# A mixer in four PSUM banks, a LayerNorm in two steps, and a build whose TensorE work is spread

## The chip, the core and the metric

The kernel runs on one core of one Trainium2 chip. It is one program for all engines: PE (TensorE) multiplies matrices, DVE (VectorE), ACT (ScalarE) and POOL (GpSimd) work on vectors, SP issues most of the transfers. The metric is the device time of one execution in microseconds (us). A profiled execution is a run of its own, and its trace gives for each instruction the start, the length, and what ended the idle time ahead of it.

## What is computed

The reference is one decoder layer on 512 prompt tokens and 32 sample tokens (8 sequences of 4), with 1,024 features, in f32. Cut to what matters:

```python
proj = x @ w_in + b_in                          # q, k, v, g, ca, cg: 512 columns each
o, r_new = retention(rope(q), rope(k), v, r0)   # 4 heads of 128, chunks of 128 tokens
ret_out = silu(g) * head_norm(o)
conv_out, buf_new = conformer_conv(ca, cg, ...) # GLU, causal convolution of width 31, LayerNorm, swish
mix = concat(ret_out, conv_out) @ w_out
x = layer_norm(ALPHA * x + mix, ln1_g, ln1_b)

q = x @ w_query                                 # 8 heads, two halves of 128 each
s1, s2 = q1 @ sub_keys_1, q2 @ sub_keys_2       # 128 keys each
v1, i1 = top_k(s1, 16);  v2, i2 = top_k(s2, 16)
sv, ci = top_k(v1[:, None] + v2[None], 16)      # 16 of 256 pairs
idx = e1 * 128 + e2;  gate = softmax(sv)        # 16 of 16,384 experts per head
act = gelu(peer_u[idx] . x)
ffn = sum(gate * act * peer_v[idx])
y = layer_norm(ALPHA * x + ffn, ln2_g, ln2_b)
```

Each token uses 8 × 16 = 128 experts. An expert has a row of `peer_u` and one of `peer_v`, 4 KB each.

## The kernel before, in words

**Two ways through the experts.** For the first two blocks of 128 prompt tokens (called `x1_0` and "b") and for the samples ("s", 32 tokens, four experts of each at once, so 32 slots instead of 128) the experts are gathered. `gather` (its generator issues one slot per step) has POOL issue an indirect DMA of 128 rows of 8 KB (L579, 1 MB), DVE takes the dot product with the token (L582), ACT the Gelu and the scale by the gate (L590, L591), and DVE adds the scaled v row to an accumulator (L596). The other 256 prompt tokens (`ND`) go through all 16,384 experts densely: for each of 128 first keys `e`, `scores_of(e)` multiplies the block `ut[e]` of 128 experts with `x1T` on PE (L801, eight f32 matmuls, two records each in the trace), ACT takes the Gelu into a tile of weights `GW`, and `v_stage(e)` multiplies the weights with the v rows into the four accumulators `pB` in PSUM (L939). The weights are zero but for the chosen experts: `build` makes, for groups of 8 tokens, one-hot matrices from the top-k's results (ACT's `off` and `A`, L879 and L881; DVE's `M` and `B`, L883 and L887), multiplies them on PE (L892, 24 bf16 matmuls for a group), and DVE multiplies the result into the weights (L916) or copies it there for keys whose scores come later (L918).

The 128 first keys are in four groups: Gb (32 keys), Gc (20), Ga (44) and Gd (32). The scores of Ga and Gb are computed ahead of the build, one key after the other, each with a PSUM tile `sp` and a Gelu of its own (L847, L852); those of Gc during the first build by `s_stage`; those of Gd during the tail.

**The stages in time.** Up to about 386 us: input projections, convolution and retention, with the first 128 tokens taken right through to their top-k, so that their gather (`gather0`) runs from then on beside everything else. 386 to 454: the mixer. Blocks of w_out are loaded as `wo`; `mix_a` multiplies (L478; `residual`, L465, adds ALPHA times x), for the 32 samples and for three blocks of 128 tokens; `mix_b` normalizes (`layer_norm`, L444 to L458: statistics on DVE, the inverse root on POOL, a scalar for the shift on DVE at L454, ACT's Identity at L456, then DVE's product with g and sum with b) and has PE transpose the result (L489) into `x1T`. PSUM is in two pools, `ps` of five banks and `ps0` of three, used alternately. Then `caches` writes the convolution's caches out (two transposes, L429 and L437, and ten stores), and 470 to 785 is the retrieval: `w_query` in four units of two heads (`project`, L198), their key scores (L524), and `retrieve` on DVE (MAX8 and its companions, L506 to L510), first for the dense tokens, then for "b" and "s". The Ga and Gb scores fill PE meanwhile, up to 857. The first slots of the "s" gather run from 786; `FREE` = 12 of them may run ahead of the `fence`, the last DVE instruction of `first_keys`. 858 to 985: `first_keys`, the first build, with one `s_stage` every 12 tokens. 985 to the end, the tail: `phases` (v rows, Gd's scores and `last_keys`, the second build) and `fetched` (the remaining slots of "s" and 128 of "b") step by step beside each other, then the last LayerNorms and stores.

**What sets the order.** The program is written against tiles; a scheduler that simulates the engines sets each engine's order, which is then fixed: every engine runs its instructions in that order and each waits for its semaphores. Pools with `bufs=` n make the n+1st tile wait for the last user of the first. `behind(a, b)` keeps an instruction after another in that order without a wait of its own. `hold(k, ins)` says that the dots of `gather0` from slot k on come after `ins`; the mixer has such holds at slots 52, 56, 60, 64 and 68.

The layer's `layer_norm` before, with the instructions that the change is about:

```python
rsqrt(rs[:n, 0:1], mv[:n, 1:2])
V.scalar_tensor_tensor(rs[:n, 1:2], mv[:n, 0:1], -1.0, rs[:n, 0:1], op0=OP.mult, op1=OP.mult)
for q, c in enumerate(halves if src else [slice(0, D)]):
    S.activation(t[:n, c], src[q][:n] if src else t[:n, c], AF.Identity, bias=rs[:n, 1:2], scale=rs[:n, 0:1])
    V.tensor_mul(t[:n, c], t[:n, c], g[:n, c])
    steps["ln"] = V.tensor_add(t[:n, c], t[:n, c], b[:n, c])
```

## Time and profile before

| | |
|---|---|
| median of 3 runs | 1592.72 us (1591.25, 1592.72, 1597.43) |
| profiled execution | 1598.13 us, span 1595.8 us |
| granted TensorE clock, mean | 0.968 |
| PE, DVE, ACT, POOL busy | 94%, 77%, 38%, 23% |
| moved by DMA | 503.75 MB, mean 316 GB/s |

A row of the timeline gives start, length, engine, line, operation, output and inputs, how many such instructions stand in a row, and in brackets the idle time ahead of it with what ended it. A row of a stretch gives its length, the busy time of each engine with the number of instructions, the granted TensorE clock, the share of time that the 16 DMA engines were busy, and GB/s. The tail's records of PE overlap slightly at their ends, so a sum of single lengths is larger than the time they take.

### The profile page before, as it was taken

What the parts mean: (1) busy time and instruction counts of PE and PEld (TensorE: products, weight loads), DVE (VectorE), ACT (ScalarE), POOL (GpSimd) and SP (SyncE); (2) the same over time, 40 slices, a digit from 0 to 9 for tenths busy, and PEclk for the clock granted to TensorE, in tenths of its full rate; (3) what the DMA queues carried; (4) which work ended last, traced back from release to release, by engine and by line L of the source; (5) the groups of instructions that cost most, each with busy time, mean ns of one, the idle gap of its engine ahead of it and who ended that gap; (6) DMA issues with size and microseconds to landing.
All of it is one profiled execution on the core that took longest, in us unless ns stands there. A gap on an engine that the chain in (4) does not pass through costs nothing.

```text
span 1595.8 us, 20861 instructions
## 1 busy us (share of the span) xinstructions
PE 1499.0 (94%) x7046; PEld 1015.8 (64%) x7046; DVE 1225.1 (77%) x3158; ACT 602.9 (38%) x1686; POOL 365.0 (23%) x335
## 2 busy tenths in 40 slices
PE   7899999997969999999899997999999999999995
PEld 6788657565856668788788885444566656543332
DVE  4939998878866999999863789656877777766666
ACT  2234353145222333333533798413994111111111
POOL 2001324333331221222120001222224222222221
PEclk9899989998989999999999997999999999999998
DMA  9458787995698779999796322998999999999995
GB/s 362 176 189 346 250 301 238 353 332 208 231 377 344 274 266 342 342 344 344 268 362 238 107 93 87 393 391 328 394 359 390 424 424 423 424 424 424 423 424 209
DMA packets 99543, 503.75 MB, mean 316 GB/s; under 512 B 10183, under 2 KB 21191, under 8 KB 56549
## 3 DMA queue, kind: packets, MB, share of 16 engines
q0 software_dynamic: 42240, 305.12, 49.1%
q1 hardware_dynamic: 50749, 189.96, 31.5%
q10 hardware_dynamic: 6448, 7.36, 1.5%
q8 instruction: 55, 0.90, 0.2%
q14 instruction: 51, 0.42, 0.1%
HBM read 497.03 MB, written 5.80 MB: 315 GB/s over the span
## 4 chain that ended last, share of the span: by engine, by line
DMA 29%; PE 28%; DVE 24%; issue 9%; ACT 7%; POOL 3%; SPq 0%; DVEq 0%; POOLq 0%; ACTq 0%
DMA g<-in_uv_dram,Ib 18%; PE sp L801 9%; DMA g<-in_uv_dram,I 7%; DVE acc L596 6%; PE pB L939 5%; PE mm L198 4%; DVE g L582 4%; ACT off L879 3%; POOL g L579 2%; PE mm L478 2%; PE mm L263 2%; DMA g<-in_w_in_dram 2%; PE mm L892 2%; ACT A L881 1%; PE mm L309 1%
## 5 line engine op out<-in xcount | busy, mean ns | idle before, releaser
L801 PE MATMUL sp<-x1T,uv 128*128 128x256 f32 x2048 | 465.0, 384 | 14.2 <-ACT Ga L847 7.1
L596 DVE SCALAR_TENSOR_TENSOR acc<-g,wgt,acc 128x1024 f32<-128x1024 f32 x285 | 364.8, 1280 | 116.6 <-ACT wgt L591 113.8
L801 PEld LDWEIGHTS sp<-x1T,uv 128*128 128x128 f32 x2048 | 385.9, 192 | 87.4 <-issue 14.9
L590 ACT ACTIVATE act<-act 128x1 f32<-128x1 f32 x288 | 57.7, 200 | 574.5 <-DVE g L582 567.9
L579 POOL DMA_INDIRECT g<-in_uv_dram,I x128 | 164.9, 1288 | 468.0 <-DVE acc L596 236.0
L582 DVE SCALAR_TENSOR_TENSOR g<-g,x1g 128x1024 f32<-128x1024 f32 x160 | 195.3, 1223 | 97.1 <-DMA g<-in_uv_dram,Ib 64.3
L579 POOL DMA_INDIRECT g<-in_uv_dram,Ib x128 | 135.9, 1062 | 498.0 <-DVE acc L596 314.8
L198 PE MATMUL mm<-x1T,w 128*128 128x384 f32 (+1 forms) x512 | 178.1, 505 | 0.0
L582 DVE SCALAR_TENSOR_TENSOR g<-g,x 128x1024 f32<-128x1024 f32 x128 | 154.9, 1215 | 26.7 <-DMA g<-in_uv_dram,I 26.5
L939 PE MATMUL pB<-uv,Ga 128*128 128x512 f32 x352 | 162.1, 603 | 0.6 <-DMA uv<-in_uv_dram 0.4
L879 ACT ACTIVATE off<-row,e1T 128x128 bf16<-128x128 bf16 x512 | 157.9, 389 | 1.0
L198 PEld LDWEIGHTS mm<-x1T,w 128*128 128x128 f32 x512 | 97.9, 193 | 72.4 <-issue 41.0
L939 PE MATMUL pB<-uv,Gd 128*128 128x512 f32 x256 | 117.2, 601 | 2.1 <-DMA uv<-in_uv_dram 1.0
L939 PE MATMUL pB<-uv,Gb 128*128 128x512 f32 x256 | 115.4, 604 | 2.0 <-DMA uv<-in_uv_dram 1.4
L939 PEld LDWEIGHTS pB<-uv,Ga 128*128 128x128 f32 x352 | 63.7, 189 | 82.9 <-issue 63.1
L939 PEld LDWEIGHTS pB<-uv,Gd 128*128 128x128 f32 x256 | 46.1, 189 | 73.3 <-issue 71.5
L892 PEld LDWEIGHTS <-A 128*128 128x128 bf16 x1536 | 64.0, 99 | 34.7 <-issue 26.0
L939 PEld LDWEIGHTS pB<-uv,Gb 128*128 128x128 f32 x256 | 47.6, 192 | 58.8 <-issue 52.6
L892 PE MATMUL mm<-B,A 128*128 128x96 bf16 (+1 forms) x1536 | 67.7, 195 | 11.2 <-DVE Gc L918 10.0
L881 ACT ACTIVATE A<-off 128x1024 bf16<-128x1024 bf16 x64 | 67.4, 1053 | 22.5 <-PE mm L892 21.7
L939 PE MATMUL pB<-uv,Gc 128*128 128x512 f32 x160 | 72.3, 599 | 0.0
L887 DVE TENSOR_TENSOR B<-M,gtT 128x768 bf16<-128x768 bf16 (+1 forms) x192 | 69.5, 415 | 3.1 <-PE mm L892 3.0
(279 smaller groups left out, 1712.4 us busy)
## 6 DMA issues: line engine op xcount, KB each, us to landing
uv<-in_ut_dram SPq DMA_DIRECT2D x128, 512.0 KB
uv<-in_uv_dram SPq DMA_DIRECT2D x128, 512.0 KB
w<-in_w_in_dram SPq DMA_DIRECT2D x18, 1024.0 KB
w<-in_w_query_dram SPq DMA_DIRECT2D x16, 1024.0 KB
w<-in_w_out_dram SPq DMA_DIRECT2D x7, 1024.0 KB
g<-in_uv_dram,I POOLq DMA_INDIRECT x128
keys<-in_state_retention_dram ACTq DMA_DIRECT2D x4, 512.0 KB
out_dram<-keys SPq DMA_DIRECT2D x4, 512.0 KB
```

What stands on the lines that cost most here:

```text
L198: T.matmul(p[:, :n], w[m // 2][:, k, (m % 2) * 128:(m % 2 + 1) * 128], xT[:, k, c0:c0 + n], start=(k == 0), stop=(k == 7))
L263: T.matmul(p[:, :L], dg[:, k % 4], u_p[:, m, p0 + k:p0 + k + L], start=(k == 0), stop=(k == CK - 1))
L579: G.indirect_dma_start(out=t, out_offset=None, in_=a["uv"], in_offset=bass.IndirectOffsetOnAxis(ap=idx[:, k:k + 1], axis=0))
L582: dot = V.scalar_tensor_tensor(t[:, :D], t[:, :D], 1.0, x1, op0=OP.mult, op1=OP.mult, accum_out=act[:, 0:1])
L590: S.activation(act[:, 1:2], act[:, 0:1], AF.Gelu)
L596: V.scalar_tensor_tensor(acc, v, wgt, acc, op0=OP.mult, op1=OP.add)
L801: T.matmul(sp, u[:, k], x1T[:, k, NG2:], start=(k == 0), stop=(k == 7))
L879: S.activation(off[:, t], row, AF.Abs, bias=e1T[:, t1 + t:t1 + t + 1])
L881: S.activation(A, off, AF.Relu, bias=1.0, scale=-1.0)
L887: V.tensor_tensor(B[:, q], M, pairs_of(gtT[:, q], t1).to_broadcast([128, TB // 2, ne, 2]), op=OP.mult)
L892: T.matmul(pt[:, t % nt], A[:, t - t1], B[:, q, (t - t1) // 2, :, t % 2], start=(q == 0), stop=(q == 2))
L939: T.matmul(pB[b][q], W[:, b * 128:(b + 1) * 128], vt[:, q * 512:(q + 1) * 512], start=False, stop=(e == NK - 1), skip_group_check=True)
```

## The change

1. **LayerNorm in two steps.** DVE computes (x − mean)·g in one instruction, straight from PSUM where the source is there, and then that times the inverse deviation plus b. L454 and ACT's Identity go. The inverse root is POOL's as before, or, with `table=True` (the "b" block's and the two dense blocks' last LayerNorms), ACT's Sqrt and DVE's reciprocal.
2. **Caches and loads.** `caches()` moves ahead of the mixer. The third block of w_out goes to the space of `u_p`, and the first unit of w_query is loaded before the mixer, partly into the space of `blk`.
3. **Mixer in four banks.** `ps` and `ps0` are closed ahead of the mixer; it has four banks (`mx`), and the other four (`pq`) hold the first query unit, computed by `first_unit` in columns 0 to 160, 160 to 288 and 288 to 416 between the mixer's pieces. `mix_b(NS, C)` now precedes `mix_a(NS + C, C, 1)`. The holds are at slots 52, 54, 56, 59 and 62.
4. **Score pairs.** For Ga and Gb one PSUM tile takes two keys' scores, and one Gelu empties it.
5. **PE's work in the first build spread.** `s_stage`'s first matmul comes behind the build's matmul of its token; a stage comes every 31/3 tokens in place of 12, and after the 20 keys of Gc come the products of four v rows with the first 128 dense tokens. Their other half follows after the fence.
6. **`FREE` from 12 to 20.** Eight more slots of "s" may run ahead of the fence.

Its core:

```diff
-        rs = gw.tile([128, 2], F32, name="lrs", bufs=3)
-        rsqrt(rs[:n, 0:1], mv[:n, 1:2])
-        V.scalar_tensor_tensor(rs[:n, 1:2], mv[:n, 0:1], -1.0, rs[:n, 0:1], op0=OP.mult, op1=OP.mult)
-        for q, c in enumerate(halves if src else [slice(0, D)]):
-            S.activation(t[:n, c], src[q][:n] if src else t[:n, c], AF.Identity, bias=rs[:n, 1:2], scale=rs[:n, 0:1])
-            V.tensor_mul(t[:n, c], t[:n, c], g[:n, c])
-            steps["ln"] = V.tensor_add(t[:n, c], t[:n, c], b[:n, c])
+        rs = gw.tile([128, 1], F32, name="lrs", bufs=3)
+        if table:
+            S.activation(rs[:n], mv[:n, 1:2], AF.Sqrt, bias=eps_c[:n])
+        else:
+            rsqrt(rs[:n], mv[:n, 1:2])
+        cs = halves if src else [slice(0, D)]
+        for q, c in enumerate(cs):
+            V.scalar_tensor_tensor(t[:n, c], src[q][:n] if src else t[:n, c], mv[:n, 0:1], g[:n, c],
+                                   op0=OP.subtract, op1=OP.mult)
+        if table:
+            V.reciprocal(rs[:n], rs[:n])
+        for c in cs:
+            steps["ln"] = V.scalar_tensor_tensor(t[:n, c], t[:n, c], rs[:n], b[:n, c], op0=OP.mult, op1=OP.add)
...
-    wo = load_w(a["w_out"], 0) + load_w(a["w_out"], 512)
+    caches()
+    spare = [u_p.rearrange("p m t -> p (m t)")[:, 0:2 * D], blk[:, 0:2 * D]]
+    spare = [t.rearrange("p (k e) -> p k e", k=8) for t in spare]
+    wo = load_w(a["w_out"], 0) + load_w(a["w_out"], 512, [spare[0], None])
...
+    wq0 = load_w(a["w_query"], 0, [None, spare[1]])
+    fps.close()
+    leftp, mxs = ExitStack(), ExitStack()
+    pq = leftp.enter_context(tc.tile_pool(name="pq", bufs=4, space=PSUM, side="right", reuse_waits="tile"))
+    mx = mxs.enter_context(tc.tile_pool(name="mx", bufs=4, space=PSUM, reuse_waits="tile"))
+    banks[:] = [mx]
+    q_first = [pq.tile([128, 512], F32, name="mm") for _ in range(4)]
+
+    def first_unit(c0, c1):
+
+        for m in range(4):
+            for k in range(8):
+                T.matmul(q_first[m][:, c0:c1], wq0[m // 2][:, k, (m % 2) * 128:(m % 2 + 1) * 128], x1T[:, k, c0:c1],
+                         start=(k == 0), stop=(k == 7), skip_group_check=True)
+
     mix_a(0, NS, None)
     mix_a(NS, C, 0)
     mix_b(0, NS)
+    hold(54, steps["ln"])
+    mix_b(NS, C)
     hold(56, steps["ln"])
     mix_a(NS + C, C, 1)
-    mix_b(NS, C)
-    hold(60, steps["ln"])
     mix_a(NS + 2 * C, C, None)
+    first_unit(0, NS + C)
     mix_b(NS + C, C)
-    hold(64, steps["ln"])
+    hold(59, steps["ln"])
+    first_unit(NS + C, NS + 2 * C)
     mix_b(NS + 2 * C, C)
-    hold(68, steps["ln"])
-    caches()
+    hold(62, steps["ln"])
+    first_unit(NS + 2 * C, n)
...
+    def scores_of(e, ne=1, after=None):
+
+        sp = pdn.tile([128, 2, ND], F32, name="sp")
+        for i in range(ne):
+            u = uvp.tile([128, D], F32, name="uv").rearrange("p (k e) -> p k e", k=8)
+            nc.sync.dma_start(u, a["ut"][e + i])
+            for k in range(8):
+                p = T.matmul(sp[:, i], u[:, k], x1T[:, k, NG2:], start=(k == 0), stop=(k == 7), skip_group_check=True)
+                if after is not None and i + k == 0:
+                    behind(p, after)
+        return sp[:, 0:ne] if ne > 1 else sp[:, 0]
...
-    for e in range(E0S[2], E0S[3]):
-        S.activation(place(e), scores_of(e), AF.Gelu)
+    for e in range(E0S[2], E0S[3], 2):
+        S.activation(place2(e), scores_of(e, 2), AF.Gelu)
...
-    for e in range(EG[0]):
-        S.activation(place(e), scores_of(e), AF.Gelu)
+    for e in range(0, EG[0], 2):
+        S.activation(place2(e), scores_of(e, 2), AF.Gelu)
...
-                if ts.stop % 12 == 0 and done < EG[1]:
-                    s_stage(E0S[1] + done, ts.stop)
+                if ts.stop != 4 * ((8 + 31 * (done + len(ahead)) // 3) // 4):
+                    continue
+                if done < EG[1]:
+                    s_stage(E0S[1] + done, ts.stop, mm)
                     done += 1
+                elif len(ahead) < UV:
+                    ahead.append(v_row(len(ahead)))
+                    behind(v_products(len(ahead) - 1, ahead[-1], 0), mm)
...
     def phases():
-        for e in range(EG[0]):
+        for e, vt in enumerate(ahead):
+            v_products(e, vt, 1)
+            yield
+        for e in range(len(ahead), EG[0]):
             v_stage(e)
             yield
```

## The prediction

> **What bounds the kernel now.** I read the busy shares first, then the busy time by stage, then within each stage the rows that end its idle time.
>
> ```profile
> span 1595.8 us, 20861 instructions
> PE 1499.0 (94%) x7046; PEld 1015.8 (64%) x7046; DVE 1225.1 (77%) x3158; ACT 602.9 (38%) x1686; POOL 365.0 (23%) x335
> ```
>
> PE's 94% is a mean; the next rows give, by stretch, busy time of PE, PE weight loads, DVE, ACT and POOL, then granted clock, DMA share and GB/s.
>
> ```profile
> 450.00:470.00 20.00, 6.95 (x38) 5.77 (x37) 12.26 (x18) 4.50 (x12) 5.89 (x6) 0.66 1.01 422
> 600.00:780.00 180.00, 175.04 (x854) 152.06 (x854) 177.18 (x691) 61.85 (x160) 39.50 (x34) 0.99 0.90 330
> 785.90:857.80 71.90, 68.92 (x331) 60.20 (x330) 35.20 (x51) 25.09 (x79) 14.51 (x13) 0.98 0.95 364
> 857.80:985.70 127.90, 116.47 (x1078) 99.92 (x1077) 101.37 (x382) 107.55 (x301) 0.00 (x0) 0.93 0.27 88
> 985.70:1587.00 601.30, 587.53 (x2288) 300.94 (x2288) 424.39 (x636) 200.74 (x633) 159.41 (x153) 0.99 0.97 391
> 1400.00:1577.00 177.00, 174.27 (x383) 68.63 (x382) 119.69 (x143) 24.14 (x97) 41.26 (x44) 1.00 0.99 412
> ```
>
> So five stages bind differently: a PE stall at 450–470; the retrieval, where PE and DVE are both 97–98% busy; the rest of the scores, on PE and DMA; the build, where PE, ACT and DVE stand at 91, 84 and 79% and POOL and the DMA engines have next to nothing; and the tail, where PE is 98% busy and DMA 97%.
>
> **Mixer and first query unit.**
>
> ```profile
> 386.43 1.06 PE L478 MATMUL mm<-w,blk 128*32 128x256 f32 x2 [5.95 <-ACT blk L300]
> 438.95 13.98 PE L478 MATMUL mm<-w,blk 128*128 128x256 f32 x64
> 466.86 1.08 PE L489 MATMUL mm<-cst,xr 128*128 128x128 f32 x4 [13.05 <-DVE xr L458]
> 479.78 12.73 PE L198 MATMUL mm<-x1T,w 128*128 128x416 f32 x36
> 129.87 3.73 PE L198 MATMUL mm<-g,w 128*128 128x128 f32 x32
> 391.52 1.51 ACT L333 ACTIVATE on<-mm,hnb,hrs 128x128 f32<-128x128 f32 x4 [1.01 <-DVE hnb L330]
> 458.32 1.23 DVE L582 SCALAR_TENSOR_TENSOR g<-g,x 128x1024 f32<-128x1024 f32 x1 [5.93 <-DMA g<-in_uv_dram,I]
> 505.93 0.93 DVE L506 MAX8 vf<-score 128x8 f32<-128x128 f32 x4 [0.90 <-ACT score L527]
> ```
>
> The mixer's matmuls run from 386.43 to 452.9, and with the transposes after them to 453.8; then PE waits 13.05 us for the last LayerNorm, of which 5.93 is DVE sitting in a gather dot whose slot had not landed. Query unit 0 ends at 492.5 and the top-k begins at 505.93. The change takes the gather out of the LayerNorms and puts three pieces of query unit 0 into those waits. It doesn't get the whole 13 us. (1) In the new order the transposes of the third retention chunk (input `on`, ready at 391.52 + 1.51 = 393.0) stand ahead of all mixer matmuls, where before the mixer filled 386.4 to 393: −7 us of the gain. (2) Four banks mean that each pair waits for the LayerNorm that reads it; one such wait, 3–4 us, stands after the second block. (3) The unit whole is 64 records in 22.5 (36 in 12.73); a piece of 128 columns is 64 in 7.5 (32 in 3.73), the one of 160 a quarter more, 9.3, so the three take 24.3. Summed from 394: two mixer blocks 30 (13.98 each and 1 to 2 of residuals), wait and transposes 4.5, two blocks 32, first piece 9.3, transposes 2, two pieces and the last transposes 16: about 488. Against 492.5 that is a gain of 4.4 (bounds −9 to +3, the whole stall less 7 against a second LayerNorm wait). The score records that PE ran between unit 0 and the first top-k are only moved, not saved: the keys' load leaves its place behind the cache outputs, so the top-k can begin near 489, 17 us early.
>
> **What DVE does with 17 us.** By the order of DVE, the new mixer holds 8 gather slots where the old held 12, and 52 to 67 rather than 52 to 77 are done when the top-k begins: 10 slots move behind it.
>
> ```profile
> L596 DVE SCALAR_TENSOR_TENSOR acc<-g,wgt,acc 128x1024 f32<-128x1024 f32 x285 | 364.8, 1280 | 116.6 <-ACT wgt L591 113.8
> L582 DVE SCALAR_TENSOR_TENSOR g<-g,x 128x1024 f32<-128x1024 f32 x128 | 154.9, 1215 | 26.7 <-DMA g<-in_uv_dram,I 26.5
> L801 PE MATMUL sp<-x1T,uv 128*128 128x256 f32 x2048 | 465.0, 384 | 14.2 <-ACT Ga L847 7.1
> 786.91 1.48 DVE L887 TENSOR_TENSOR B<-M,gtT 128x768 bf16<-128x768 bf16 x3
> ```
>
> A slot is 1.22 + 1.28 = 2.5 us of DVE: 10 are 25. With DVE full in the retrieval, its chain comes to the build's first operands (before at 786.91) not 17 earlier but 25 − 17 = 8 us later.
>
> **Score pairs.** One Gelu for two keys lets PE run a pair ahead. PE's waits from 470 to 860, by what it waited for (total, times, longest):
>
> ```profile
> PE sp L801 <- ACT Ga L847: 7.1, 5, 3.1
> PE sp L801 <- ACT Gb L852: 4.7, 2, 3.0
> 857.80 0.29 DVE L916 TENSOR_TENSOR Gb<-Gb,mm 128x128 f32<-128x128 f32 x1 [12.11 <-ACT Gb L852]
> 844.40 1.28 DVE L596 SCALAR_TENSOR_TENSOR acc<-g,wgt,acc 128x1024 f32<-128x1024 f32 x1 [0.66 <-ACT wgt L591]
> ```
>
> If all 11.8 goes, PE ends the second group near 857.8 − 4.4 − 11.8 = 841. But DVE, which had 12.11 us of room before its first multiply at 857.80, comes 8 later: its twelfth slot of the s gather ends near 845.7 + 8 = 854, and the multiply follows it. The DMA engines at 0.95 cannot pull those slots in. The build therefore starts at about 853, −5 (bounds −16, both gains whole, to +4, a slot's landing later each).
>
> **Build.**
>
> ```profile
> 861.67 4.55 PE L801 MATMUL sp<-x1T,uv 128*128 128x256 f32 x20
> 866.05 1.20 PE L892 MATMUL mm<-B,A 128*128 128x96 bf16 x24
> 867.09 4.55 PE L801 MATMUL sp<-x1T,uv 128*128 128x256 f32 x20
> 899.29 0.29 DVE L916 TENSOR_TENSOR Gb<-Gb,mm 128x128 f32<-128x128 f32 x1 [1.89 <-PE mm L892]
> 973.62 2.08 PE L892 MATMUL mm<-B,A 128*128 128x96 bf16 x24 [2.23 <-DVE Gc L918]
> 966.00:985.00 19.00, 10.57 (x142) 9.61 (x143) 18.29 (x72) 18.71 (x51) 0.00 (x0) 0.64 0.01 2
> 857.80:985.70 127.90, 7.86 (x16) 2.71 (x16) 0.93 0.27 88
> L591 ACT ACTIVATE wgt<-act,GTb 128x1 f32<-128x1 f32 x128 | 37.4, 292 | 3.5
> 985.75 8.47 PE L939 MATMUL pB<-uv,Gb 128*128 128x512 f32 x16 [0.38 <-DVE Gb L916]
> ```
>
> The first groups of 8 tokens take 5.42 us (861.67 to 867.09) with PE the bound and DVE idle 1.89 in each; at the end DVE and ACT are busy 18.3 and 18.7 of 19 us, and PE waits in each group. Spreading the key scores evens this; the ideal would be the busiest engine's sum. That was PE's 116.5 of 127.9. The change adds 8 slots, 8 × 2.5 = 20, to DVE: 101.4 + 20 = 121.4; ACT gets a Gelu and a scale for each, 8 × 2 × 0.29 = 4.7 at most, 112. Four half rows of value products (16 records, as in the row of L939 in the build, 7.86 us) change nothing: the build already held 16. So DVE becomes the longest, and its queue is in order: each dot waits for its slot, each acc for two ACT instructions behind the `off` chain (0.66 in the row of 844.40), and the multiplies behind them hold the PSUM bank from PE. I take 10% over 121.4, as 127.9 stands 10% over 116.5: 134 and a slot's landing at the front, 135, +7 (bounds −4, 124, to +15, 143). The fence then falls at 853 + 135 = 988, some 2 us after 985.7.
>
> **Tail.** 8 slots fewer of 148. At 1 MB each (128 rows of 8 KB) and the 412 GB/s of 1400–1577 they are 8 × 1.05/0.412 = 20 us of DMA. PE doesn't follow:
>
> ```profile
> 985.70:1587.00 601.30, 459.04 (x1008) 183.98 (x1008) 0.99 0.97 391
> L892 PE MATMUL mm<-B,A 128*128 128x32 bf16 x768 | 24.4, 176 | 0.3 <-ACT A L881 0.3
> 1576.43 3.60 PE L939 MATMUL pB<-uv,Gd 128*128 128x512 f32 x8
> 1577.33 1.29 DVE L603 SCALAR_TENSOR_TENSOR yt<-x1g,acc 128x512 f32<-128x512 f32 x2
> 1586.93 1.45 ACT L456 ACTIVATE g<-pB,lrs 128x512 f32<-128x512 f32 x2 [2.77 <-DVE lrs L454]
> 1589.02 1.28 DVE L458 TENSOR_TENSOR g<-g,lnb 128x512 f32<-128x512 f32 x2
> ...
> 388.27 1.28 ACT L590 ACT_TABLE_LOAD   x1
> ```
>
> The first row is L939 alone in the tail: 1,008 records, whose 459 us overlap at their ends; at 8 in 3.60 less that overlap, 0.44 each, they are 444. With 24.4 for the second build and 512 score records (32 keys) at 4.38/20 = 0.22, 113, PE needs about 582 of the 594.3 us to the last matmul at 1580.0. So at most 12.3 comes back. Part of PE's idle is the tail's first rows and the join at its end, not the DMA: −9 (bounds −12.5 to −3).
>
> **End.** From 1577.33 to 1590.3 DVE alternates the LayerNorm of the last gathered block with the two dense ones, the last store ends the span 5.5 later. With DMA 20 us lighter, the gathered block ends before PE, and each dense block sheds ACT's Identity pair (1.45): −4.5 (bounds −6 to 0, a table load being the charge against it). A Sqrt needs a table other than Gelu's; a load takes the 1.28 of the row of 388.27, and can stand in the chain once, if the statistics don't cover it.
>
> The Trainium skill ("ScalarE: Activation LUTs", What ACT_TABLE_LOAD costs) adds a drain of some 1.38 us to such a load; the row agrees on the load and shows no drain by itself; by the page the end would gain 3.1 rather than 4.5.
>
> **The sum.** −5 + 7 − 9 − 4.5 = −11.5 us against the profiled execution's own 1598.1 (span 1595.8 and 2.3 around it): 1586.6. The median shown, 1592.72, stands 5.4 below that execution, so I give 1592.7 − 11.5 = 1581.
>
> **Rivals.**
> (a) Everything carries: the top-k's early start is not eaten because DVE waits less for slots (the row of L582 shows 26.5 us of DMA waits), the pairs give 10, the build stays at 128 and the tail gives 12: −10 − 4.4 − 12 − 4 ≈ −30, 1562. For it: PE's records are a fixed sum, and its idle is what the change removes. Against it: DVE's 177.18 of 180.
> (b) The change doesn't arrive at the end: the 25 us on DVE eat front and pairs (start 857), the build takes 138 and the tail returns 8: 0 + 10 − 8 − 3 ≈ −1, 1592. For it: the DVE sum of 121.4 and a tail that is PE's.
> (c) Slower: the build becomes a chain of waits. A gather dot in DVE's queue that waits for its slot holds the multiplies, PE idles in each group, and the granted clock falls, as in 966–985 (clock 0.64, 24 records 2.08 in place of 1.20). A group with a key score then needs up to 16 × 0.22 × 2.08/1.20 = 6.1 for it and 2.1 for its own matmuls, against 3.5 and 1.2; if the 20 such groups take 5.4 and the other 12 DVE's 121.4/32 = 3.8, the build is 154, +26; with −5 − 6 − 3 that is +12, 1605. It decides from a build of 127.9 + 14 + 8 = 150 on. For it: DVE becomes the longest engine and PE idles between groups; against it: the stage's mean clock of 0.93, of which its last 19 us at 0.64 leave (0.93 × 127.9 − 0.64 × 19)/108.9 = 0.98 for the rest, where the groups hold key scores.
>
> The Trainium skill ("TensorE: Matmul & The Clock Gate", Part 1: The HAM clock gate) says that TensorE's full clock has to be held by activity and that an idle window of about 3.4 us halves it. The trace agrees in direction: 0.66 beside the 13.05 us stall, 0.64 where waits of 1 to 2 us recur, though none of those is 3.4 long. By the page's threshold alone (c) would not arise from waits that short; the rows say that it can.
>
> **How the numbers follow.** The sum above: 0.46, and its own range 1574 to 1589; (a) 0.20; (b) 0.18; (c) 0.16. A difference below 0.5%, 8 us, is what a measurement of this kernel can just tell from none: 1584.7 to 1600.7 is no change. The sum's case lies below 1584.7 in 0.39 of its 0.46, (a) wholly: faster 0.59. The other 0.07 and (b)'s 0.16 are no change, 0.23; (c) and 0.02 of (b) slower, 0.18. For eight in ten the range runs from 1560, below (a), to 1602, which leaves out most of (c).
>
> **What the profile after would show.** Right: no wait above 5 us between mixer and query unit 0, its end near 488; MAX8 of the dense top-k near 490; no waits of L801's scores on Ga and Gb; the first Gb multiply at 850–855 behind a gather dot; 32 build groups of about 4.2 us; a fence at 985–990; last matmul near 1572, and 11 us behind it. Wrong: a build over 150 or under 128; a first multiply before 846 (then DVE was not the bound) or after 860; a tail shorter than 582, which would say that its PE work was smaller than I summed.

## The result, and the profile after

The changed kernel takes 1600.12 us (median of 7 runs, 1597.67 to 1605.91) against 1592.72 for the kernel before (7 runs, 1589.28 to 1601.61): a ratio of 1.0056, 95% interval 1.003 to 1.0081. Forecast were 1581 us and a gain. The profiled execution of the changed kernel took 1605.57 us, its span is 1603.6. The lines of the changed file are shifted: L939 is now L950, L801 is L833, L892 is L926, L582 is L590, L590/L591 are L598/L599, L596 is L604, L916/L918 are L966/L968, L900 is L935 and L903 is L938.

The stretches of the changed kernel that answer to those shown of before (length; busy time of PE, PE weight loads, DVE, ACT, POOL; granted clock, DMA share, GB/s):

```profile
450.00:470.00 20.00, 20.00 (x112) 18.40 (x112) 14.71 (x22) 1.99 (x8) 3.78 (x4) 1.00 0.51 191
600.00:780.00 180.00, 173.25 (x850) 151.27 (x849) 176.66 (x661) 68.36 (x158) 43.81 (x36) 0.99 0.95 351
859.30:1000.70 141.40, 120.02 (x1077) 101.11 (x1075) 118.10 (x398) 111.38 (x316) 8.39 (x8) 0.94 0.42 145
1000.70:1590.00 589.30, 582.72 (x2279) 300.43 (x2280) 398.75 (x599) 195.74 (x617) 161.70 (x139) 1.00 0.95 385
```

The stall at 450–470 is gone. The retrieval moves more (351 GB/s, before 330) with DVE as full as before. The build is 13 us longer, and no engine fills it: PE is busy for 120 of 141 us and DVE for 118. The tail stands where it stood.

For the comparison of stages I take four marks from each trace: ACT's `on` of the third retention chunk (391.52 before, 392.05 after), DVE's first multiply of the build into Gb, the first value product released by DVE behind the build (the fence), and the end of the last matmul. They don't depend on where the front began, which differs by up to 9 us between executions.

| us | on to Gb multiply | build | fence to last matmul | behind it |
|---|---|---|---|---|
| before | 466.3 | 128.0 | 594.3 | 15.8 |
| changed | 467.2 | 141.5 | 593.4 | 9.5 |
| difference | +0.9 | +13.5 | −0.9 | −6.3 |
| predicted | −5 | +7 | −9 | −4.5 |

With the 0.5 by which `on` came later the differences add to the 7.8 between the two spans.

The ends of PE's waits in the changed kernel, from 380 to 990 (total, times, longest):

```profile
PE mm L341 <- ACT on L334: 11.3, 1, 11.3
PE mm L926 <- DVE Gc L968: 10.1, 8, 3.1
PE mm L779 <- ACT x1T L498: 4.4, 1, 4.4
PE mm L868 <- DVE e L862: 4.0, 1, 4.0
PE sp L833 <- ACT act L598: 3.9, 1, 3.9
PE mm L926 <- ACT A L915: 3.8, 2, 2.6
PE sp L833 <- ACT Ga L881: 2.7, 2, 1.8
PE mm L497 <- DVE keys L466: 2.6, 1, 2.6
...
```

PE stands 11.3 us at the head of the mixer for `on`, then 2.6 for a LayerNorm (L497), 4.4 for the copy of the transposed blocks that the second piece of query unit 0 reads (L779), 4.0 for the dense top-k's result (L868), which DVE finishes late, and 3.9 and 2.7 for a score's PSUM tile that ACT has not emptied yet. Before, the list had 13.1 us for the last LayerNorm, 11.8 for the Gelus of scores and 6.0 at the head of the mixer. The first and the last went and the second fell to 6.6, but the new waits are about as long as what was saved.

And inside the build, DVE's waits of the changed kernel from 861.9 to 1000:

```profile
DVE Gc L938 <- ACT W L935: 18.0, 7, 4.8
DVE Gb L966 <- PE mm L926: 4.7, 6, 1.5
DVE acc L604 <- ACT wgt L599: 0.6, 1, 0.6
```

The 18.0 us are new. DVE waits here for no gather slot, and only 0.6 us in a slot's chain; it waits for W, the Gelu of a key score.

### The profile page after: what moved, and what is told of

Read it like the earlier page. It is cut to its first block, busy times and chain, and to the rows that moved or that the text cites. A ratio compares the mean times of both kernels' runs of the same rounds, so it can differ in the third digit from the quotient of the medians.

```text
span 1603.6 us, 20993 instructions
## 1 busy us (share of the span) xinstructions
PE 1501.4 (94%) x7174; PEld 1030.4 (64%) x7174; DVE 1222.3 (76%) x3143; ACT 587.9 (37%) x1636; POOL 377.4 (24%) x329
## 4 chain that ended last, share of the span: by engine, by line
PE 54%; DVE 27%; DMA 10%; issue 5%; ACT 3%; POOL 2%; SPq 0%; DVEq 0%; POOLq 0%; ACTq 0%
PE pB L950 27%; PE sp L833 12%; DVE acc L604 6%; DVE g L590 5%; DMA g<-in_uv_dram,I 4%; PE mm L486 4%; PE mm L199 3%; PE mm L926 2%; PE mm L264 2%; DMA g<-in_w_in_dram 2%; POOL g L587 1%; PE mm L310 1%; DVE iu L518 1%; DVE B L921 1%; DVE score L516 1%
## 5 line engine op out<-in xcount | busy, mean ns | idle before, releaser
L833 PE MATMUL sp<-x1T,uv 128*128 128x256 f32 x2048 | 472.3, 389 | 10.2 <-ACT act L598 3.9
L833 PEld LDWEIGHTS sp<-x1T,uv 128*128 128x128 f32 x2048 | 392.2, 195 | 85.6 <-issue 25.3
L604 DVE SCALAR_TENSOR_TENSOR acc<-g,wgt,acc 128x1024 f32<-128x1024 f32 x285 | 364.2, 1278 | 108.0 <-ACT wgt L599 106.5
L598 ACT ACTIVATE act<-act 128x1 f32<-128x1 f32 x288 | 57.6, 200 | 628.6 <-DVE g L590 622.3
L587 POOL DMA_INDIRECT g<-in_uv_dram,Ib x128 | 150.6, 1177 | 439.1 <-DVE acc L604 290.2
L590 DVE SCALAR_TENSOR_TENSOR g<-g,x1g 128x1024 f32<-128x1024 f32 x160 | 195.0, 1221 | 53.9 <-DMA g<-in_uv_dram,Ib 37.8
L590 DVE SCALAR_TENSOR_TENSOR g<-g,x 128x1024 f32<-128x1024 f32 x128 | 154.5, 1212 | 26.1 <-DMA g<-in_uv_dram,I 25.4
L950 PE MATMUL pB<-uv,Ga 128*128 128x512 f32 x352 | 162.2, 604 | 0.3
L199 PE MATMUL mm<-x1T,w 128*128 128x384 f32 (+1 forms) x448 | 153.3, 498 | 0.0
L199 PEld LDWEIGHTS mm<-x1T,w 128*128 128x128 f32 x448 | 84.5, 190 | 60.7 <-issue 28.6
L950 PE MATMUL pB<-uv,Gb 128*128 128x512 f32 x256 | 116.1, 606 | 5.0 <-DMA uv<-in_uv_dram 3.0
L950 PEld LDWEIGHTS pB<-uv,Ga 128*128 128x128 f32 x352 | 63.7, 190 | 83.8 <-issue 63.0
L950 PE MATMUL pB<-uv,Gd 128*128 128x512 f32 x256 | 114.8, 599 | 0.9
L950 PEld LDWEIGHTS pB<-uv,Gd 128*128 128x128 f32 x256 | 47.0, 190 | 68.7 <-issue 50.4
L926 PEld LDWEIGHTS <-A 128*128 128x128 bf16 x1536 | 61.4, 96 | 43.9 <-issue 22.7
L950 PEld LDWEIGHTS pB<-uv,Gb 128*128 128x128 f32 x256 | 47.9, 192 | 59.7 <-issue 52.6
L926 PE MATMUL mm<-B,A 128*128 128x96 bf16 (+1 forms) x1536 | 65.3, 192 | 18.3 <-DVE Gc L968 10.1
L950 PE MATMUL pB<-uv,Gc 128*128 128x512 f32 x160 | 72.8, 601 | 0.0
```

Source lines behind the costliest of these rows:

```text
L199: T.matmul(p[:, :n], w[m // 2][:, k, (m % 2) * 128:(m % 2 + 1) * 128], xT[:, k, c0:c0 + n], start=(k == 0), stop=(k == 7))
L587: G.indirect_dma_start(out=t, out_offset=None, in_=a["uv"], in_offset=bass.IndirectOffsetOnAxis(ap=idx[:, k:k + 1], axis=0))
L590: dot = V.scalar_tensor_tensor(t[:, :D], t[:, :D], 1.0, x1, op0=OP.mult, op1=OP.mult, accum_out=act[:, 0:1])
L598: S.activation(act[:, 1:2], act[:, 0:1], AF.Gelu)
L604: V.scalar_tensor_tensor(acc, v, wgt, acc, op0=OP.mult, op1=OP.add)
L833: p = T.matmul(sp[:, i], u[:, k], x1T[:, k, NG2:], start=(k == 0), stop=(k == 7), skip_group_check=True)
```

## The experiments

Each ratio is to runs of the kernel before that were taken with the run's own (medians 1593.7 to 1595.6 us). Lengths of stages come from one profiled execution of each version.

### The build: the slots, or the places of the key scores

Twelve slots in place of 20 ahead of the fence, all else as changed:

```diff
-FREE = 20
+FREE = 12
```

> The changed kernel with 12 instead of 20 slots of the s gather allowed ahead of the fence; all else as changed. In the changed kernel the build takes 141 us from the first Gb multiply (859.3) to the fence (1000.7), before 128. Theory A (the 8 slots lengthen the build by their DVE time): the build falls to 125-129, the tail, which PE bounds, stays at 593 us from fence to last matmul, the time is 1586 to 1589, against 1600 as changed. Theory B (the key scores' new places lengthen it: DVE waits 18.0 us there for W, ACT 18.4 us for PE): the build stays at 134 or more, the time is 1594 or more.

Measured: ratio to before 1.0044 (1.0027 to 1.0061), build 136.2 us, tail 593.8, end 14.7. In these two profiles the slots cost 141.5 − 136.2 = 5.3 us of build, and without them the end behind the last matmul is 5.2 longer: their account is even. DVE's waits for W are 28.2 us here against 18.0, so the slots' 20 us of DVE partly fill time in which it waits anyway.

The old places of the key scores, 20 slots:

```diff
-                if ts.stop != 4 * ((8 + 31 * (done + len(ahead)) // 3) // 4):
-                    continue
-                if done < EG[1]:
-                    s_stage(E0S[1] + done, ts.stop, mm)
+                if ts.stop % 12 == 0 and done < EG[1]:
+                    s_stage(E0S[1] + done, ts.stop)
                     done += 1
-                elif len(ahead) < UV:
-                    ahead.append(v_row(len(ahead)))
-                    behind(v_products(len(ahead) - 1, ahead[-1], 0), mm)
```

> The changed kernel with the old first build: a key score every 12 tokens with no tie to the build's matmuls, no v products ahead; 20 slots stay. Theory A (slots): the build stays at 136 to 142 us, the time at 1597 to 1602. Theory B (places of the key scores): the build falls to 126-130 although the slots are in it, DVE's waits for W go from 18 us to under 4, the time is 1586 to 1590.

Measured: ratio 0.9972 (0.9945 to 0.9999), build 130.7 us. Both edits together:

> The changed kernel with the old first build and 12 slots: only the two-step LayerNorm, the mixer with query unit 0, and the pairs are left of the change. Both theories: the build is back at 126-129 us, the fence at 986-988, the tail 593, the end 9.5 us after it as in the changed kernel (15.8 before): 1586 to 1588, faster than before by 5. If the time is at or above that of before, the front part of the change costs more than its first Gb multiply (859.3 against 857.8) shows.

Measured: ratio 0.9967 (0.9947 to 0.9988), build 125.2, tail 592.8, end 14.7. The end was expected at 9.5; what sets it is told under "End". The places of the key scores cost 141.5 − 130.7 = 10.8 us with 20 slots and 136.2 − 125.2 = 11.0 with 12. That the two agree so closely is partly luck, since the same build differs by up to 2.7 us between profiles. The table has every profile of this record with the old or the spread places and with none or all of the eight slots inside the build (the other edits of these runs lie outside it; the runs not yet named are told below):

| build, us | none of the 8 slots | all 8 |
|---|---|---|
| old places | 127.9 (before), 125.2 (both edits), 125.9 (pairs alone) | 130.7 (old places), 129.6 (the same with moved gating) |
| spread places | 136.2 (12 slots), 137.9 (light DVE), 137.9 (96 slots of the first gather) | 141.5 (changed), 140.0 (moved gating), 140.5 (32 slots of "b") |

In the runs with a light DVE and with 96 slots of the first gather, all 20 slots were done ahead of the build. By the means the places cost 11.0 and 10.5 us, and the slots 3.8 and 3.3. Theory B holds, and slots and places add. How the places cost is seen in one stretch of the changed kernel, by engine, PE first:

```profile
931.88 0.68 PE L926 MATMUL mm<-B,A 128*128 128x96 bf16 x12 [2.61 <-ACT A L915]
932.40 5.37 PE L833 MATMUL sp<-x1T,uv 128*128 128x256 f32 x16
937.60 1.19 PE L926 MATMUL mm<-B,A 128*128 128x96 bf16 x24
```

```profile
931.83 2.44 ACT L913 ACTIVATE off<-row,e1T 128x128 bf16<-128x128 bf16 x8
937.80 0.28 ACT L935 ACTIVATE W<-sp 128x132 f32<-128x132 f32 x1 [3.53 <-PE sp L833]
938.38 1.06 ACT L915 ACTIVATE A<-off 128x1024 bf16<-128x1024 bf16 x1
```

```profile
933.16 0.18 DVE L968 COPY Gc<-mm 128x32 f32<-128x32 f32 x1
938.11 0.30 DVE L938 TENSOR_TENSOR Gc<-Gc,W 128x132 f32<-128x132 f32 x1 [4.77 <-ACT W L935]
938.99 1.48 DVE L921 TENSOR_TENSOR B<-M,gtT 128x768 bf16<-128x768 bf16 x3
```

PE begins a key score at 932.40. W stands in ACT's order and its product in DVE's right behind the group's multiplies, ahead of `A` and `B` of a later group. ACT idles 3.53 us and DVE 4.77 until PE has finished that one score. While they stand, nothing is made for a later group, and PE waits in turn for `A` or for DVE's copy out of PSUM (2.61 us here for `A`, 2.58 for the copy ahead of the score at 956.59). Behind such a wait the score itself is slower, 5.37 against 3.68 for the same 16 records. Five of the 20 key scores are, each behind a wait of PE of 1.6 to 3.1 us; together they lose 7.4. The granted clock (third number from the end) shows it, in the wait, in the score's first 3.5 us, and behind the score:

```profile
929.25:931.88 2.63, 0.02 (x2) 0.03 (x2) 2.63 (x12) 2.57 (x8) 0.00 (x0) 1.00 0.60 198
932.40:935.90 3.50, 3.50 (x13) 2.85 (x11) 0.76 (x5) 1.87 (x7) 0.00 (x0) 0.55 0.02 7
937.60:940.00 2.40, 2.40 (x32) 2.25 (x31) 1.89 (x8) 2.04 (x5) 0.00 (x0) 1.00 0.47 147
```

To see whether it is the nearness or the spreading, the spread places were kept and only the use of a score was put one stage later:

```diff
-                if ts.stop != 4 * ((8 + 31 * (done + len(ahead)) // 3) // 4):
+                if ts.stop != 4 * ((8 + 31 * (done + len(pend) + len(ahead)) // 3) // 4):
                     continue
+                if pend:
+                    s_use(*pend.pop(), ts.stop)
+                    done += 1
                 if done < EG[1]:
-                    s_stage(E0S[1] + done, ts.stop, mm)
-                    done += 1
+                    pend.append((E0S[1] + done, scores_of(E0S[1] + done, 1, mm)))
```

Here `s_use` is the rest of `s_stage`, the Gelu and the product, and `pend` holds the score that is not used yet.

> The changed kernel with the key scores of the first build where it has them (tied behind the build's matmuls, spread), but their Gelu and the product with the weights one stage, some 10 tokens, later. Theory B in its narrow form (DVE's and ACT's waits for a score that PE has only just begun are what costs): DVE's waits for W fall from 18 us to under 4 and the build from 141.5 to 129-132, ratio 0.997 to 0.999. Theory G (the cost is PE's: a score between the groups holds the next group's matmuls and the idle in between lowers its clock): the build stays at 137 or more, ratio 1.003 to 1.006.

Measured: build 130.5 us, ratio 0.9987 (0.9957 to 1.0017) against 1.0056. The stretch of the build of this run:

```profile
858.00:988.50 130.50, 113.77 (x1078) 96.10 (x1076) 117.73 (x398) 110.79 (x316) 8.95 (x8) 0.99 0.46 158
```

DVE's and ACT's sums are those of the changed kernel (118.1 and 111.4 there), PE's is 6 lower at a clock of 0.99 in place of 0.94, and one key score of the 20 is slow in place of five. DVE's list of waits has no line for W any more. Theory B in its narrow form holds: what cost 11 us was that the use stood right behind the score. The slow scores are part of that price. The clock alone does not tell it: the kernel before has 0.93 with a build of 128.

The Trainium skill ("TensorE: Matmul & The Clock Gate", Part 1: The HAM clock gate) has TensorE's clock fall to half behind an idle window of about 3.4 us and return after as long of work. The rows agree in the size of the loss (5.37 − 3.68 = 1.69, half of 3.4), but here idle times of 1.6 to 3.1 us were enough (waits of 1.2 us, at 868.88 and 903.28, were not followed by a slow score).

### The front

The gating of the third chunk (`gate_heads`, which has PE transpose `on`) behind the samples' mixer block and in the mixer's banks:

```diff
-    gate_heads(ons[3], C, gT, NS + 2 * C)
     wq0 = load_w(a["w_query"], 0, [None, spare[1]])
...
     mix_a(0, NS, None)
+    gate_heads(ons[3], C, gT, NS + 2 * C)
     mix_a(NS, C, 0)
```

> The changed kernel with the third chunk's gating transposes written behind the samples' mixer block and in the mixer's banks, so that PE's 11.3 us wait for them ahead of the mixer can go. Theory C (PE bounds the scores up to the first Gb multiply, which waited 5.2 us for the last Gelu): query unit 0 ends near 487 in place of 494.6, the first Gb multiply comes 5 to 7 earlier, the time falls by as much, 1593 to 1595. Theory D (DVE's chain of top-k and gather bounds that stage): query unit 0 ends earlier but the first Gb multiply stays within 2 us, the time at 1598 to 1601.

Measured: ratio 1.0016 (0.9996 to 1.0036), 460.8 us from `on` to the Gb multiply, 6.4 less, and the mixer begins at 387.15. This agrees with theory C. One profile says little about a few us here: the six profiles with this front as changed have 465.3 to 467.2, the four with moved gating and nothing else moved in the mixer 455.9 to 464.1, 5.6 less on the mean. The wait for `on` was worth about what the prediction put on it (7).

The pairs alone, on the kernel before (`pair_of` puts two keys' scores into one tile and empties it with one Gelu):

```diff
-    for e in range(E0S[2], E0S[3]):
-        S.activation(place(e), scores_of(e), AF.Gelu)
+    for e in range(E0S[2], E0S[3], 2):
+        pair_of(e)
...
-    for e in range(EG[0]):
-        S.activation(place(e), scores_of(e), AF.Gelu)
+    for e in range(0, EG[0], 2):
+        pair_of(e)
```

> The kernel before with the score pairs alone. In it PE waits 11.8 us for the Gelus of Ga and Gb and DVE has 12.1 us of room at the first Gb multiply, which comes 466.3 us after the third chunk's 'on' (391.52 to 857.80). Theory E (the pairs' gain is real and was used up in the changed kernel by DVE's 10 later gather slots): 6 to 9 us less from 'on' to the first multiply, the time 6 to 9 below before, ratio 0.994 to 0.996. Theory F (PE only waits elsewhere, for v rows, for DVE or in ACT's queue): within 2 us, ratio 0.999 to 1.001.

Measured: ratio 0.9975 (0.9955 to 0.9996), but 465.9 us from `on` to the multiply against 466.3. PE's waits of this run from 470 to 860:

```profile
PE sp L802 <- ACT Ga L811: 6.0, 3, 4.7
PE sp L802 <- ACT Gb L811: 3.8, 1, 3.8
PE sp L802 <- DMA uv<-in_ut_dram: 1.9, 1, 1.9
```

The waits for Gelus are 9.8 us, where before they were 11.8, and 1.9 for a row of keys came in. By stages theory F is right; the 0.25% of the whole lies elsewhere (build 125.9, tail 591.8), and its cause was not followed up. Why the waits stay is seen in ACT's order in this run, ahead of PE's waits of 4.70 that ends at 660.23 and of 3.77 that ends at 817.57:

```profile
656.20 0.20 ACT L590 ACTIVATE act<-act 128x1 f32<-128x1 f32 x1 [5.76 <-DVE g L582]
656.43 0.29 ACT L591 ACTIVATE wgt<-act,GT 128x1 f32<-128x1 f32 x1
656.75 1.28 ACT L562 ACT_TABLE_LOAD   x1
658.04 0.23 ACT L562 ACTIVATE ex<-ex 128x32 f32<-128x32 f32 x1
658.29 1.28 ACT L811 ACT_TABLE_LOAD   x1
659.58 0.60 ACT L811 ACTIVATE Ga<-sp 128x512 f32<-128x512 f32 x1
```

```profile
813.37 0.29 ACT L591 ACTIVATE wgt<-act,GTs 128x1 f32<-128x1 f32 x1
816.82 0.20 ACT L590 ACTIVATE act<-act 128x1 f32<-128x1 f32 x1 [3.15 <-DVE g L582]
816.93 0.58 ACT L811 ACTIVATE Gb<-sp 128x512 f32<-128x512 f32 x1
```

In both the Gelu of the scores stands behind a gather slot's Gelu, which waits for DVE's dot (5.76 and 3.15 us). In the first, two loads of ACT's function table stand between them as well, 1.28 us each, around an Exp of the retrieval's softmax (L562). In these two waits, 8.5 of the 9.8 us, it was not the Gelu's own length (0.60) that PE waited for, and one Gelu for two keys stands in the same queue.

The holds of the mixer's slots set back, all else as changed:

```diff
-    hold(54, steps["ln"])
+    hold(56, steps["ln"])
...
-    hold(56, steps["ln"])
+    hold(60, steps["ln"])
...
-    hold(59, steps["ln"])
+    hold(64, steps["ln"])
...
-    hold(62, steps["ln"])
+    hold(68, steps["ln"])
```

> The changed kernel with the slots that wait for the mixer's LayerNorms set at 56, 60, 64 and 68 again, so that more gather slots are done before the top-k starts. In the changed kernel two PE waits come of a late DVE or of a slot: 4.0 us for the dense top-k's result, 3.9 in ACT's queue behind a gather's Gelu. If the 10 slots moved behind the top-k are what takes the front's gain, the wait for the dense result goes, 'on' to first Gb multiply falls from 467.2 to 461-463, ratio 1.002 to 1.003. If the slots hold the LayerNorms up instead, the last piece of query unit 0 ends later than 494.6 and the multiply stays within 2 us, ratio 1.005.

Measured: 467.0 us, ratio 1.0041 (1.0017 to 1.0065). The wait for the dense top-k fell from 4.0 to 2.6 and that in ACT's queue from 3.9 to none, but the waits for Gelus of Ga and Gb grew from 2.7 (Ga alone) to 4.6 and 2.0. From 470 to the multiply PE's waits add to 15.0 us in both kernels. Query unit 0 ended as in the changed kernel. The multiply stayed as the second answer has it, but not for its reason: no LayerNorm was held up.

What sets it was tried by taking load away. First DVE's, in the changed kernel:

```diff
-            dot = V.scalar_tensor_tensor(t[:, :D], t[:, :D], 1.0, x1, op0=OP.mult, op1=OP.mult, accum_out=act[:, 0:1])
+            dc = 128 if x1 is x1_0 and k >= 64 else D
+            dot = V.scalar_tensor_tensor(t[:, :dc], t[:, :dc], 1.0, x1[:, :dc], op0=OP.mult, op1=OP.mult, accum_out=act[:, 0:1])
```

and the sum over the same `dc` columns.

> The changed kernel in which the first block's gather slots from 64 on take their dot product and their sum over 128 instead of 1,024 columns (those experts' parts are left out of the first block's output): DVE has some 64 x 2 us less to do from the top-k's start to the first Gb multiply, the transfers are the same. In the changed kernel 'on' to that multiply is 467.2 us. If DVE's time sets the stretch (the prediction's step), it falls by 8 us or more, to 459 or less. If transfers or PE set it, it stays at 464 to 468.

Measured: 464.9 us, 2.3 less, ratio 1.001 (0.9983 to 1.0037). Then slots with their transfers:

```diff
-    gather0 = gather(x1_0, I0, g0_gates, acc0, range(PH * TK))
+    gather0 = gather(x1_0, I0, g0_gates, acc0, range(96))
```

> The changed kernel with 96 of the first block's 128 gather slots (32 experts of each of its tokens left out): 32 MB less, 75 us of transfers at 424 GB/s, and 80 us less of DVE, between the top-k's start and the first Gb multiply. If the transfers set the stretch, 'on' to multiply falls by 8 us or more while the run with a light DVE stays; if both fall alike, it is DVE; if neither falls by more than 4, PE's own order sets it.

Measured: 457.6 us, 9.6 less, ratio 0.9951 (0.9916 to 0.9985). The two runs from 600 to 780, the light DVE first, then the 96 slots:

```profile
600.00:780.00 180.00, 174.36 (x863) 152.26 (x864) 107.62 (x536) 68.01 (x173) 43.24 (x41) 0.97 0.95 364
```

```profile
600.00:780.00 180.00, 175.14 (x873) 152.93 (x872) 151.73 (x613) 63.84 (x144) 23.52 (x24) 0.98 0.73 267
```

With DVE at 108 of 180 us and DMA at 0.95, PE does 863 records here (850 in the changed kernel); with DMA at 0.73 it does 873, although its busy share is the same. A full DVE does not bound the stretch: 69 us less of it here brought 2.3. By the marks set down, it would be the transfers, of which 34 MB, 79 us at 424 GB/s, bought 9.6. But the slots left out are work of ACT and POOL too, and PE's waits say more. From 470 to the multiply they are 15.0 us in the changed kernel, 13.2 with the light DVE and 9.7 with 96 slots; those for Gelus fall from 6.6 to 0.9 and 1.1. So PE bounds the stretch, by its records and its waits: 1.8 of the 2.3 us and 5.3 of the 9.6 are waits that went. That the transfers by themselves set the rest is not shown.

### The tail

Without the last 96 slots of the "b" gather:

```diff
-            yield from gather(x1g, Ig[g], GTg[g].rearrange("p h k -> p (h k)"), ac, range(128 // r_))
+            part_of = gather(x1g, Ig[g], GTg[g].rearrange("p h k -> p (h k)"), ac, range(128 // r_))
+            for _ in range(32):
+                next(part_of)
+                yield
```

> The changed kernel without the last 96 of the b gather's 128 slots (the second prompt block gets 32 of its 128 experts): 100 MB less for the DMA engines in the tail, PE's work as it was. Fence to last matmul was 594.3 us before and 593.4 in the changed kernel. If PE's work there is 582 us, as the prediction summed it, and the rest its waits for transfers, it falls to 582-584. If PE is the bound throughout (its busy time there is 586.8), it stays at 586 to 589 and 8 slots could never give back 9 us.

Measured: 568.6 us from fence to last matmul, one execution (1572.63 us). That is below both answers. A stretch of the kernel before, with slots, and one of this run, without:

```profile
1285.70:1385.70 100.00, 98.37 (x328) 60.00 (x328) 71.47 (x95) 18.43 (x67) 25.32 (x27) 1.00 1.02 424
```

```profile
1292.75:1392.75 100.00, 100.00 (x347) 65.63 (x346) 6.37 (x15) 5.76 (x15) 0.00 (x0) 1.00 0.44 153
```

In the first, 424 GB/s carry a row of 0.52 MB and a slot of 1.05 MB in 3.71 us. In the second, 153 GB/s carry rows alone, one in 3.42. How PE goes through two rows, one of keys and one of values, is seen in these rows, the kernel before first:

```profile
1300.89 3.69 PE L801 MATMUL sp<-x1T,uv 128*128 128x256 f32 x16
1304.46 3.70 PE L939 MATMUL pB<-uv,Ga 128*128 128x512 f32 x8
1308.27 3.69 PE L801 MATMUL sp<-x1T,uv 128*128 128x256 f32 x16
```

```profile
1299.96 3.60 PE L950 MATMUL pB<-uv,Ga 128*128 128x512 f32 x8
1303.39 3.62 PE L833 MATMUL sp<-x1T,uv 128*128 128x256 f32 x16
1306.85 3.60 PE L950 MATMUL pB<-uv,Ga 128*128 128x512 f32 x8
```

From start to start, 16 score records take 3.57 us with slots and 3.46 without, 8 value records 3.81 and 3.43. PE counts as busy in both, because a value record is 0.60 us long while the next one starts 0.43 behind it when nothing holds it (3.43/8); the first 0.17 us of a wait do not show as idle time. Without slots nothing holds PE, and its own work in the tail comes out as 32 × 3.46 for the scores, 126 × 3.43 for the values and 24.4 for the second build, 567 us, against 568.6 measured. So a slot costs the tail 3.71 − 3.42 = 0.29 us, and 96 slots cost (593.4 − 568.6)/96 = 0.26 each.

### Versions that use the findings

The old build with moved gating, 20 slots, and the same with 16:

> The changed kernel with the old first build and with the third chunk's gating transposes behind the samples' mixer block, 20 slots. If the two gains add: 461 us from 'on' to the first Gb multiply, 130-131 for the build, 593 for the tail to the last matmul, 9.5 behind it, ratio to before 0.993 to 0.995. If the earlier start only moves slots' landings into the build, the build takes 134 or more and the ratio is 0.997.

> As the run with the old build and the moved transposes, with 16 slots ahead of the fence in place of 20. In the changed kernel the b gather's LayerNorm ended 29 us ahead of the last matmul, in the run with 12 slots together with it; a slot of the tail takes about 3.7 us. So 16 should keep the short end (9.5) and give back half of the 5.4 us that 8 slots cost in the build: build 128, ratio 0.0015 below the run with 20. If the slots' cost in the build is a matter of their landing at the front of it alone, 16 and 20 are the same within 1 us.

Measured: 0.9946 (0.9919 to 0.9973), with 455.9, 129.6, 594.3 and 9.5 us; and 0.9918 (0.9889 to 0.9947), with 464.1, 126.1, 593.6 and 9.5. The two have the same front in the text, so the first stretch varies by some 8 us between such executions or orders. With 16 slots the end stays short, and the build is 3.5 us shorter in this pair of profiles.

Transposes of the second-last block ahead of query unit 0's first piece, with 16 slots and moved gating, once with the old build and once with the late use:

```diff
-    first_unit(0, NS + C)
     mix_b(NS + C, C)
     hold(59, steps["ln"])
+    first_unit(0, NS + C)
```

> The changed kernel with the old first build, 16 slots, the third chunk's gating behind the samples' mixer block, and the second-last block's transposes ahead of query unit 0's first piece, which covers their copy. PE's wait of 4 to 6 us for that copy (4.43 in the changed kernel) goes; build 126, tail 593, end 9.5. If PE bounds the scores: 4 less from 'on' to the multiply than the 461 of the run with the moved gating, ratio to before 0.989 to 0.992. If waits further on take it back: 0.992 to 0.995.

> As the run with the old build, 16 slots, moved gating and moved transposes, but with the changed kernel's spread key scores, used one stage later. If spreading has a gain of its own once nothing waits for a score just begun, the build is below 126 us, 122 to 125, and the ratio 0.001 to 0.003 lower than that run's. If old and spread places are worth the same (130.5 and 130.7 with 20 slots), within 1 us.

Measured: 0.9987 (0.9964 to 1.001), with 464.5, 129.4, 596.5; and 0.9957 (0.9934 to 0.998), with 467.4, 122.5, 592.7. The wait for the copy fell to 0.2 in both, and 4.9 and 4.4 us appeared ahead of the first key scores (L532) instead, for which the profile names no releaser: nothing gained. In the build, spread scores with late use are 6.9 us shorter than the old places, with two slots inside the build in each. With all eight inside, late use (130.5) is no better than the old places (130.7 and 129.6).

Gating moved, 16 slots, spread scores with late use, without moved transposes:

> The changed kernel with the third chunk's gating behind the samples' mixer block, 16 slots ahead of the fence, and the spread key scores used one stage later. From the runs so far: 'on' to multiply 461 to 464, build 123 to 126, tail 593, end 9.5: ratio to before 0.990 to 0.994, as good as the run with the old places and 16 slots (0.9918) or better. If the late use needs the moved transposes to be worth anything: 0.995 or more.

Measured: 1578.43 us median of 6 runs, ratio 0.9885 (0.985 to 0.9919), with 461.3, 124.2, 593.0 and 9.5. This version beats both kernels: with three edits (moved gating, 16 slots, late use) the changed kernel is 1.1% faster than the kernel before, 0.8 to 1.5 by the interval.

## Why the prediction was wrong, point by point

**The sum.** It was −5 + 7 − 9 − 4.5 = −11.5; the profiles give +0.9 + 13.5 − 0.9 − 6.3, and 0.5 ahead of it. Three terms carry the miss, the tail by 8 us, the build by 6.5 and the front by 6. The time of 1600.12 us lies inside the range of 1560 to 1602, whose upper end was there for rival (c); the forecast was a gain, and a loss came.

**Mixer.** The steps were right: the wait for `on` (11.3 seen, 7 of it predicted as loss; moving it gave 6.4), and a LayerNorm wait after the second block (2.6). Missing was the wait of the second piece for the copy of the transposes, 4.4; the mixer's blocks took some 2 us more than summed. Query unit 0 ended at 494.6 and not 488, the top-k began at 495.5 and not 489. The copy stood in ACT's queue behind a gather slot's Gelu, which waited for DVE:

```profile
477.38 0.20 ACT L598 ACTIVATE act<-act 128x1 f32<-128x1 f32 x1 [5.89 <-DVE g L590]
477.62 0.29 ACT L599 ACTIVATE wgt<-act,GT 128x1 f32<-128x1 f32 x1
477.82 0.58 ACT L498 ACTIVATE x1T<-mm 128x512 f32<-128x512 f32 x1
```

**"What DVE does with 17 us" and the pairs.** Two steps failed: "If all 11.8 goes, PE ends the second group near ... 841", and with it "DVE, which had 12.11 us of room before its first multiply at 857.80, comes 8 later ... and the multiply follows it". DVE ended its last slot ahead of the multiply at 852.79 + 1.29 = 854.1, as predicted (854), and then waited for PE:

```profile
852.79 1.29 DVE L604 SCALAR_TENSOR_TENSOR acc<-g,wgt,acc 128x1024 f32<-128x1024 f32 x1 [1.19 <-ACT wgt L599]
859.28 0.29 DVE L966 TENSOR_TENSOR Gb<-Gb,mm 128x128 f32<-128x128 f32 x1 [5.20 <-ACT Gb L886]
```

That DVE was right is luck. In the traces 75 dots of the first gather stand ahead of the first MAX8 of the dense top-k before the change and 68 after it, so 7 slots moved behind it and not 10, and the top-k began 10.4 us earlier and not 17: 7 × 2.5 − 10.4 = 7 in place of 25 − 17 = 8.

PE came 17 us after the 841 that the prediction gave it, and its waits account for that. Query unit 0 ended 6.6 us later than predicted, and from there on PE waited 4.0 for the top-k's result and 6.6 for Gelus, where the prediction had nothing: 841 + 6.6 + 10.6 = 858, and the Gelu of the last scores of Gb starts at 858.65. What it had wrong is that the 11.8 us were the Gelus' own. They were ACT's queue, in which the Gelus stand behind gather slots and table loads, and pairs alone left 9.8 of them. "With DVE full in the retrieval" was read off 177.18 of 180 us; the run with a light DVE shows that full is not the same as bounding.

**Build.** "DVE becomes the longest, and its queue is in order" gave +7; the slots do cost time of that kind, 3 to 5 us. The step that failed is "Spreading the key scores evens this": it counted sums of engines and left out that each score's Gelu and product stand in ACT's and DVE's order right behind the score. That is 11 us, and the use one stage later returned it. Whether spreading then evens the build is open: with 16 slots late use has 122.5 and 124.2 us against 126.1 and 129.4 with the old places, but with 20 slots the two are alike. Rival (c) had the mechanism's outline, in-order waits, PE's idle time and its clock, but put the wait at the gather's dots, and its point of decision, 150 us, supposed that the tail would pay.

**Tail.** The step "PE needs about 582 of the 594.3 us ... So at most 12.3 comes back ... −9" failed in size, and its picture too. PE's own work is 567 us: the value records follow each other in 0.43 us and not 0.44, which is 12 us over the 1,008 of them. So more than 12.3 could come back, yet a slot less returns 0.26 us, not 1.05/0.412 = 2.5, because PE itself needs 3.42 of the 3.71 us that row and slot take together. For 8 slots that is 2 us; 0.9 was measured, and single tails differ by more (592.0 to 595.4 with 20 slots ahead of the fence, 591.8 to 594.3 with 12). The same transfers that were 20 us by the DMA engines were thus almost free where they were, and cost 3 to 5 us in the build.

**End.** Right in sign, −6.3 for −4.5, inside the bounds but for 0.3. But its cause is mainly one of the two named, the slots. With 12 slots and the two-step LayerNorm the end is 14.7 in both runs, so the LayerNorm gives 1.1 and the gathered block's earlier end the other 5.2. The table load stood far ahead of the last matmul, which ended at 1594.1:

```profile
1562.00 1.28 ACT L456 ACT_TABLE_LOAD   x1 [4.16 <-DVE lmv L453]
1593.48 0.29 ACT L456 ACTIVATE lrs<-lmv,eps_c 128x1 f32<-128x1 f32 x1 [29.89 <-DVE lmv L453]
```

By the Trainium skill ("ScalarE: Activation LUTs", What ACT_TABLE_LOAD costs) the charge was 2.66 us for a switch, 1.38 of it a drain; here it was hidden whole. The trace shows no such drain elsewhere either: in the pairs-only run the Exp at 658.04 starts 1.32 us after the end of the instruction ahead of its load (656.43 + 0.29).

## What to carry to other kernels

When work is spread over a loop, its consumer has to be moved back as far as its producer was moved up: on engines that run in order, a product behind a score just begun stops everything behind it, and here one stage of distance was worth 11 us. What a transfer costs is read as the difference of two paces in its own stage (3.71 against 3.42 us a row), not as its bytes over the rate (2.5); and a wait named after an engine's instruction is often a wait for what stands ahead of it in that engine's queue.

## What was not expected of the hardware

PE's busy share says little about who paces it: in the tail it was 98% busy at 3.71 us a row and 100% at 3.42, at the same granted clock of 1.00. And idle times of 1.6 to 3.1 us were enough to make the next key score 1.1 to 1.7 us longer, at a granted clock of 0.55 for 3.5 us, where idle times of 1.2 us were not.
